# A second scratch bank in the half-product pairs, and token sums and squares spread over more of the down stage

## The chip, the cores and the metric

The kernel runs on one core of a Trainium2 chip. The metric is device time in microseconds (us) of one execution. A core has engines that each work through a queue of their own in order and wait for each other by semaphores: PE (TensorE) multiplies matrices and accumulates in PSUM, DVE (VectorE), ACT (ScalarE) and POOL (GpSimd) work on rows of 128 partitions, and SP (SyncE) does nothing here but issue DMA transfers. PSUM has eight banks of 128 x 512 float32 values.

## The reference, cut to what matters

The reference is one decoder layer on 512 tokens of width 1024: two token mixers (RWKV-7 and a sparse attention), their gated merge, and a feed-forward part. The change touches the feed-forward part alone, whose width D_FF is 2816:

```python
h = rms_norm(x, norm_ffn_pre)
u = causal_dwconv(h @ ffn_up, ffn_conv_w, ffn_conv_b)    # width 3, 2 x 2816 columns
u_gate, u_val = jnp.split(u, 2, axis=-1)
x = x + rms_norm((jax.nn.silu(u_gate) * u_val) @ ffn_down, norm_ffn_post)
```

Everything is float32 and agrees with the reference to float32's precision. To get this out of PE's faster number format, each operand is split into a high part and a low part (the rest), and a product is three matmuls: high by high, high by low, low by high.

## The kernel before

**The up stage** makes the 5632 columns of `h @ ffn_up` in 22 pairs j of two blocks of 128 columns, one of the gate and one of the value. Pairs 0 to 9 are plain products. Pairs 10 to 21 (`SEVEN`) go through `seven(j)`: the 2 x 2 grid of half-size products (two halves of the weights' rows and columns, two halves of the tokens) is made with seven products in place of eight. In it `prod` issues one product of 12 matmuls of 128 x 256 (line 1567), and `add` is a DVE operation (line 1572). Three PSUM banks hold a pair: g and v, which become the two blocks, and t, a scratch bank. With their numbers, the seven products go to: 1 g left, 2 t left, 3 v right, 4 t right, 5 g left (added to the first), 6 g right, 7 t right (added to the fourth). Between them DVE forms the sums: after product 2 the first one, `su` = t left - (copy of g left), by which t left is read for the last time; later v right = t right + `su4` after product 4; and v left = t right + `su` after product 7.

The tiles `pz` have two banks, used in turn; before the change a pair takes one of them, so that pairs 10, 12, 14 ... use one bank and 11, 13, 15 ... the other. Waits between engines on PSUM are kept by bank: a matmul into t right waits until a DVE operation that reads t left is done.

After each pair come the convolution on ACT and DVE (lines 1619 to 1621), SiLU, the product of both blocks, and the split of the result into `ah` (high, ACT) and `al` (low, DVE). The weights of later pairs are loaded by SP, and split by ACT (high, line 134) and POOL or DVE (low, line 172, tiles `sw...h` and `sw...l`), in program order between the rest.

**The down stage** does `@ ffn_down` for 256 tokens and 512 columns at a time, again with seven products in place of eight, m = 0 to 6. A call of `down(m, f, r, n, bank, side)` is one product: 11 steps k, each with one block of weights (loaded by SP and split by ACT, line 1668, and by DVE or POOL, line 1669) and six matmuls of 128 x 512 (lines 1733 to 1735). The blocks are numbered through: block dw(11 m + k) is step k of product m. A block is prepared ten steps ahead of its use. What runs beside the products is drawn in at the steps:

- `turn()` forms the token sums in place of the tokens as soon as these have been used. It is a generator with 15 steps: three loads of t24 from DRAM (1 MB, 1 MB and 0.75 MB; t24 was made in the up stage), then for each of three pieces (`TCH`: blocks 0 to 3, 4 to 7, 8 to 10) a difference of two DVE operations into `tt` (lines 1714, 1715) and a `put` (a copy on ACT, line 1701, and a rest on DVE, line 1702); then six more `put`s out of t24. The table `TURN` names, for each product m, the steps k that draw the next one.
- `side` is a second generator, drawn at each step k > 6: `copies` under product 1, `first_half` under product 2, `second_half` under product 5. `first_half(p2)` adds to the two banks of product 1 (line 1754), multiplies each with the norm's gain (`res`, line 1386), and takes its squares' sum on ACT (`p2jk`, line 1388), all through `stat`.
- Order is fixed by the program: what `keep` wraps is not moved by the scheduler, and every engine's queue is in order. So what a step draws in stands on DVE and ACT ahead of the weights' split of the block that is prepared there, ten steps ahead.

The token sums of rows 0, left, that the three pieces make are read by product 5; the first six `put`s out of t24 make what products 4 and 6 read.

Of the kernel before, what the change touches and what calls it, by code (L numbers as in the profile page):

```python
# [10 lines left out]
F32 = mybir.dt.float32  # L11
F32R = mybir.dt.float32r
AF = mybir.ActivationFunctionType
# [20 lines left out]
DCH = tuple(slice(i, min(i + 2, KH)) for i in range(0, KH, 2))  # L34
TURN = ((), (3, 8, 9), (0, 1, 3, 5, 7, 9), (2, 5, 8), (2, 5, 8), (), ())
TCH = (slice(0, 4), slice(4, 8), slice(8, 11))
# [16 lines left out]
def hybrid_layer(ctx: ExitStack, tc: tile.TileContext, a, out, dbg=None, stop=None):  # L53
# [33 lines left out]
    def pz(name):  # L87
        return pzs[-1][1].tile([128, 512], F32, tag="pz", name=name, bufs=2)
# [311 lines left out]
    p2 = lp[2]  # L400
# [1078 lines left out]
    with pool("ff") as ff:  # L1479
# [78 lines left out]
        def seven(j):  # L1558
# [14 lines left out]

            g, v, t = (pj if j % 2 else px)(f"sg{j}"), (pj if j % 2 else py)(f"sv{j}"), pz(f"st{j}")
            u2, u4 = (sw.tile([128, 256], F32, tag=f"u{i}", name=f"su{i}{j}", bufs=1) for i in (2, 4))
            prod(g[:, lft], tok(0, 0))
            prod(t[:, lft], forms[1])
            sc.activation(u2, g[:, lft], AF.Copy)
            add(u2, t[:, lft], u2, OP.subtract)
            prod(v[:, rgt], forms[0])  # L1580
            add(u4, v[:, rgt], u2)
            prod(t[:, rgt], forms[2])
            prod(g[:, lft], tok(1, 0), first=False)
            add(v[:, rgt], t[:, rgt], u4)
            prod(g[:, rgt], tok(1, 1))
            add(g[:, rgt], g[:, rgt], u4, OP.subtract)
            prod(t[:, rgt], forms[3], first=False)
            add(v[:, lft], t[:, rgt], u2)
            return g, v
# [90 lines left out]
        with pool("ep") as ep:  # L1680
# [23 lines left out]
            def turn():  # L1704
                def load(c):
                    keep(sy.dma_start(t24[:, c], t24d[c].rearrange("k p f -> p k f")))

                load(TCH[0])
                yield
                load(TCH[1])  # L1710
                yield
                for c in TCH:
                    x = ep.tile([128, 4, 256], F32, tag="tt", name=f"tt{c.start}", bufs=1)[:, :c.stop - c.start]
                    keep(ve.tensor_tensor(x, tok(ah, 0, 0, c).bitcast(F32), t24[:, c, lft], op=OP.subtract))
                    keep(ve.tensor_tensor(x, x, tok(al, 0, 0, c).bitcast(F32), op=OP.add))
                    yield
                    put(x, 0, 0, c)
                    yield
                    if c is TCH[0]:
                        load(TCH[2])  # L1720
                        yield
                for c in TCH:
                    put(t24[:, c, lft], 0, 1, c)
                    yield
                for c in TCH:
                    put(t24[:, c, rgt], 1, 0, c)
                    yield
# [8 lines left out]

            def down(m, f, r, n, bank, side=iter(())):
                p = [bank(f"dn{m}{i}") for i in range(2)]
                for k in range(KH - TL if m == 6 else KH):
# [5 lines left out]
                    if k % 3 == 0:  # L1745
                        next(ws, None)
                    if k > 6:
                        next(side, None)
# [12 lines left out]
            def first_half(p):  # L1761
                keep(sy.dma_start(g3, a["norms"][3:4, :].to_broadcast([128, D])))
                for i in range(2):
                    keep(add(p[i], p[i], pa[i]))
                    yield
                    s2[i] = stat(p[i], res2, i, g3, "p2", ep)
                    yield
# [13 lines left out]
            p5 = down(2, 0, 0, 1, pz, first_half(p2))  # L1781
            p4 = down(3, 3, 1, 1, pj)
            p = down(4, 1, 0, 1, px)
# [115 lines left out]
```

## Time and profile before

| | |
|---|---|
| median of 3 runs | 1147.31 us (1145.96 to 1150.28) |
| the profiled execution's own time | 1146.95 us |
| span in the profile, first to last instruction | 1144.9 us |
| mean granted TensorE clock | 0.998 |
| DVE, ACT, POOL busy | 747.6, 640.1, 608.5 us |
| chain that ended last: PE's share | 80% |
| DMA moved | 208.33 MB |

The span is divided into stages by the lines that PE executes. The twelve pairs in seven products run from 902.6 us to 1026.9 us, the down products from there to 1137.3 us, and what is left is the last norm and the stores. A row of the timeline has start, duration, engine, line, operation, the tile written and the tiles read, and in brackets the engine's idle time before it and what ended that. A row of the waits has who waited for whom, the sum in us, how many times, and the longest.

### The profile page before, as it was taken

The numbers are of one execution on the slowest core, as the hardware profiler recorded it, in microseconds if no ns is written. First come the engines' busy times: TensorE is split into PE (matmuls) and PEld (weight loads), VectorE is DVE, ScalarE is ACT, GpSimd is POOL, SyncE is SP. The second block draws the span as 40 slices with busy tenths as digits, with TensorE's granted clock in tenths as the row PEclk, the third lists the DMA queues.
The fourth block names the chain that finished last, engine by engine and source line by source line (L and its number), as shares of the span: only waits on it lengthen the run. The fifth ranks groups of instructions, "written<-read, shape, count | busy, mean of one in ns | idle before, by whom it ended". The sixth has DMA issues, their size and how long they took to land.

```text
span 1144.9 us, 21224 instructions
## 1 busy us (share of the span) xinstructions
PE 1116.2 (97%) x7704; PEld 910.2 (79%) x7704; DVE 747.6 (65%) x1432; ACT 640.1 (56%) x1258; POOL 608.5 (53%) x615
## 2 busy tenths in 40 slices
PE   9999999999999999999999999999999999999897
PEld 7888888877888877766677777888888889998685
DVE  4227664735665552597786754754885699997876
ACT  5547763554666334486665653543544666664644
POOL 4346674535666453476446544540677766753321
PEclk9999999999999999999999999999999999999999
DMA  7534468633666896426576556685658768968583
GB/s 240 149 86 123 139 168 212 180 102 96 177 144 169 233 256 207 113 71 194 170 209 181 126 126 200 212 289 146 176 160 215 223 223 230 265 185 310 168 288 117
DMA packets 117002, 208.33 MB, mean 182 GB/s; under 512 B 37025, under 2 KB 39905, under 8 KB 110754
## 3 DMA queue, kind: packets, MB, share of 16 engines
q1 hardware_dynamic: 93538, 144.05, 40.2%
q0 software_dynamic: 7504, 48.50, 18.3%
q10 hardware_dynamic: 15856, 14.42, 4.0%
q8 instruction: 61, 1.00, 0.4%
q14 instruction: 43, 0.35, 0.1%
HBM read 179.60 MB, written 72.35 MB: 220 GB/s over the span
## 4 chain that ended last, share of the span: by engine, by line
PE 80%; DVE 7%; DMA 4%; POOL 3%; issue 3%; ACT 2%; DVEq 0%; POOLq 0%; ACTq 0%; SPq 0%
PE sg L1567 4%; PE st L1567 4%; PE o L1218 3%; PE gt L348 3%; PE pt L150 3%; PE ub L1276 3%; PE pu L234 2%; PE gt L349 2%; PE ub L1278 2%; PE gt L350 2%; PE pu L233 2%; PE pu L232 2%; PE ub L1277 2%; PE v L348 2%; PE v L349 2%
## 5 line engine op out<-in xcount | busy, mean ns | idle before, releaser
L1166 ACT ACTIVATE p<-p,stt 128x384 f32<-128x384 f32 (+3 forms) x128 | 70.6, 554 | 33.5 <-DVE stt L1164 33.0
L1164 DVE CUSTOM_DVE_ANT_0 p<-s,rh 128x384 f32<-128x384 f32 (+3 forms) x128 | 59.2, 484 | 22.0 <-PE s L1150 18.4
L1734 PE MATMUL dn<-hl,ah 128*128 128x512 f32 x148 | 58.4, 394 | 2.1 <-DVE hl L1669 1.3
L1138 POOL TENSOR_SCALAR p<-p,stt 128x512 f32<-128x512 f32 (+1 forms) x64 | 39.7, 628 | 38.7 <-DVE stt L1131 23.9
L1735 PE MATMUL dn<-hh,al 128*128 128x512 f32 x148 | 57.7, 390 | 0.0
L1733 PE MATMUL dn<-hh,ah 128*128 128x512 f32 x148 | 56.4, 391 | 1.1 <-ACT hh L1668 1.1
L150 PE MATMUL pt<-ident,p 128*128 128x128 f32 x320 | 44.3, 273 | 1.3 <-DVE p L1140 1.2
L1157 PE MATMUL s<-kst,qs 128*128 128x512 f32 (+1 forms) x128 | 38.8, 394 | 6.4 <-DVE stt L1164 6.2
L150 PEld LDWEIGHTS pt<-ident,p 128*128 128x128 f32 x320 | 37.8, 141 | 7.1 <-DVE p L1140 1.6
L1218 PE MATMUL o<-PT,vt 128*64 128x384 f32 (+3 forms) x256 | 41.0, 443 | 0.0
L1734 PEld LDWEIGHTS dn<-hl,ah 128*128 128x128 f32 x148 | 27.8, 188 | 10.6 <-DVE hl L1669 3.6
L1733 PEld LDWEIGHTS dn<-hh,ah 128*128 128x128 f32 x148 | 27.6, 188 | 7.6 <-ACT hh L1668 2.0
L1157 PEld LDWEIGHTS s<-kst,qs 128*128 128x128 f32 x128 | 21.2, 189 | 15.5 <-DVE stt L1164 12.3
L1209 ACT ACTIVATE PT<-pt 128x512 f32<-128x512 f32 x48 | 27.5, 588 | 10.5 <-PE pt L150 10.3
L1140 DVE TENSOR_SCALAR p<-p,stt 128x512 f32<-128x512 f32 (+1 forms) x64 | 31.8, 524 | 0.7
L1735 PEld LDWEIGHTS dn<-hh,al 128*128 128x128 f32 x148 | 27.8, 188 | 5.5
L1218 PEld LDWEIGHTS o<-PT,vt 128*64 128x64 f32 x256 | 16.3, 136 | 18.3 <-issue 16.0
L272 POOL DMA_DIRECT2D ds<-in_down_dram x36 | 25.6, 711 | 7.6 <-DMA ds<-ds 7.6
L1620 DVE SCALAR_TENSOR_TENSOR u<-pu,cvec,u 128x511 f32<-128x511 f32 x20 | 15.0, 748 | 20.4 <-ACT u L1619 20.4
L1211 DVE COPY PT<-pt 128x512 f32<-128x512 f32 x32 | 21.8, 680 | 8.6 <-PE pt L150 8.5
L251 POOL DMA_DIRECT2D fs<-in_up_dram x36 | 26.1, 731 | 0.5 <-issue 0.4
L868 ACT ACTIVATE UV<-xs 64x256 f32<-64x256 f32 x16 | 6.1, 378 | 35.6 <-PE xs L861 35.2
(2203 smaller groups left out, 4237.8 us busy)
## 6 DMA issues: line engine op xcount, KB each, us to landing
fs<-in_up_dram POOLq DMA_DIRECT2D x36, 512.0 KB, 6.3
ds<-in_down_dram POOLq DMA_DIRECT2D x30, 512.0 KB, 6.3
fs<-fs POOLq DMA_DIRECT2D x12, 512.0 KB, 4.6
ds<-ds POOLq DMA_DIRECT2D x10, 512.0 KB, 5.5
gtd<-gt ACTq DMA_DIRECT2D x16, 256.0 KB, 4.5
qs<-qd SPq DMA_DIRECT2D x32, 128.0 KB, 4.3
g<-gtd SPq DMA_DIRECT2D x16, 256.0 KB, 3.6
t24d<-t SPq DMA_DIRECT2D x10, 256.0 KB, 5.4
```

The lines of the kernel that those rows point to most:

```text
L150: return te.transpose(o, i, ident)
L348: te.matmul(p, wh(k), hh[:, k, :], start=k == 0, stop=False)
L349: te.matmul(p, wh(k), hl[:, k, :], start=False, stop=False)
L1138: po.tensor_scalar(o.pe[e, b, k], o.pe[e, b, k], w, 1.0, op0=OP.mult, op1=OP.mult)
L1157: m = te.matmul(s_[:, :n], qt, kt[:, x, b, :n], start=x == 0, stop=x == 1)
L1164: ve.tensor_tensor_reduce(sb, parts[b], rh[e][:, (3 - qb) * 128:], -1.0, BIG, OP.add, OP.min, st[e][:, 0, i:i + 1])
L1166: sc.activation(sb, sb, AF.Exp, scale=-1.0, bias=st[e][:, 0, i:i + 1], accum_out=st[e][:, 1, i:i + 1])
L1218: te.matmul(acc[e * 64:e * 64 + 64, j * 128:], vt[:, j, b * 256 + g * 64:b * 256 + g * 64 + 64], m[e][:, c:c + n], start=False, stop=k == ...
L1567: te.matmul(p, w[y][:, ks], x[z][:, k, :], start=first and k + n == 0, stop=last and k == hf - 1 and n == 2, skip_group_check=True)
L1733: te.matmul(p, xh, w[0], start=first, stop=False)
L1734: te.matmul(p, xh, w[1], start=False, stop=False)
L1735: te.matmul(p, xl, w[0], start=False, stop=last)
```

## The change

In `seven` the scratch tile t becomes two tiles, t[0] for product 2 and t[1] for products 4 and 7, each a bank. Both banks of `pz` are now used by every pair.

In the down stage, `turn()` has another order: the difference and the `put` of the third piece (blocks 8 to 10) come after the first three `put`s out of t24 instead of before them. `TURN` draws the steps later: the first and second load under down product 1 at k = 6 and 10 instead of 3 and 8; the first piece's difference under product 2 at k = 1 instead of under product 1 at k = 9; the third load under product 2 at k = 5 instead of 1; the third piece's difference under product 3 at k = 9 and its `put` under product 4 at k = 1, instead of under product 2 at k = 7 and 9. The adds of `first_half` are made in one step and its two multiplications in two; the squares leave it and are drawn by a new generator, `squares`, under product 3 from k = 0 on. No operation is added or left out.

```diff
-TURN = ((), (3, 8, 9), (0, 1, 3, 5, 7, 9), (2, 5, 8), (2, 5, 8), (), ())
+TURN = ((), (6, 10), (1, 4, 5, 6, 10), (2, 5, 8, 9), (1, 3, 6, 9), (), ())
...
-            g, v, t = (pj if j % 2 else px)(f"sg{j}"), (pj if j % 2 else py)(f"sv{j}"), pz(f"st{j}")
+            g, v, t = (pj if j % 2 else px)(f"sg{j}"), (pj if j % 2 else py)(f"sv{j}"), [pz(f"st{j}{i}") for i in range(2)]
             prod(g[:, lft], tok(0, 0))
-            prod(t[:, lft], forms[1])
+            prod(t[0][:, lft], forms[1])
             sc.activation(u2, g[:, lft], AF.Copy)
-            add(u2, t[:, lft], u2, OP.subtract)
+            add(u2, t[0][:, lft], u2, OP.subtract)
             prod(v[:, rgt], forms[0])
             add(u4, v[:, rgt], u2)
-            prod(t[:, rgt], forms[2])
+            prod(t[1][:, rgt], forms[2])
             prod(g[:, lft], tok(1, 0), first=False)
-            add(v[:, rgt], t[:, rgt], u4)
+            add(v[:, rgt], t[1][:, rgt], u4)
             prod(g[:, rgt], tok(1, 1))
             add(g[:, rgt], g[:, rgt], u4, OP.subtract)
-            prod(t[:, rgt], forms[3], first=False)
-            add(v[:, lft], t[:, rgt], u2)
+            prod(t[1][:, rgt], forms[3], first=False)
+            add(v[:, lft], t[1][:, rgt], u2)
...
+                def diff(c):
+                    x[c.start] = y = ep.tile([128, 4, 256], F32, tag="tt", name=f"tt{c.start}", bufs=1)[:, :c.stop - c.start]
+                    keep(ve.tensor_tensor(y, tok(ah, 0, 0, c).bitcast(F32), t24[:, c, lft], op=OP.subtract))
+                    keep(ve.tensor_tensor(y, y, tok(al, 0, 0, c).bitcast(F32), op=OP.add))
...
+                diff(c0)
+                yield
+                put(x[c0.start], 0, 0, c0)
+                yield
+                load(c2)
+                yield
+                diff(c1)
+                yield
+                put(x[c1.start], 0, 0, c1)
+                yield
                 for c in TCH:
                     put(t24[:, c, lft], 0, 1, c)
                     yield
+                diff(c2)
+                yield
+                put(x[c2.start], 0, 0, c2)
+                yield
...
-            def down(m, f, r, n, bank, side=iter(())):
+            def down(m, f, r, n, bank, side=iter(()), at=7):
...
-                    if k > 6:
+                    if k >= at:
                         next(side, None)
...
                 for i in range(2):
                     keep(add(p[i], p[i], pa[i]))
+                yield
+                for i in range(2):
+                    keep(ve.tensor_tensor(res2[:, i, :], p[i], g3[:, 0:512], op=OP.mult))
                     yield
-                    s2[i] = stat(p[i], res2, i, g3, "p2", ep)
+
+            def squares(p):
+                for i in range(2):
+                    s2[i] = ep.tile([128, 3], F32, tag="p2ss", name=f"p2ss{i}", bufs=4)
+                    junk = ep.tile([128, 512], F32, tag="p2jk", name=f"p2jk{i}", bufs=1)
+                    keep(sc.activation(junk, p[i], AF.Square, accum_out=s2[i][:, 0:1]))
                     yield
...
-            p4 = down(3, 3, 1, 1, pj)
+            p4 = down(3, 3, 1, 1, pj, squares(p2), 0)
```

The order of the instructions on the engines shows this at three places. The first is PE in pair 11; the rows are the first matmul of products 2 to 7, `st` is the scratch tile (its number tells one tile from another), sg and sv are g and v. Before:

```order
L1567 MATMUL st_10122<-tf1h,sw112h 128x256
...
L1567 MATMUL sv_10121<-tf0h,sw111h 128x256 [waits Activation_49]
...
L1567 MATMUL st_10122<-tf2h,sw113h 128x256 [waits DVE_49]
...
L1567 MATMUL sg_10120<-hh,sw116h 128x256 [waits Activation_49]
...
L1567 MATMUL st_10122<-tf3h,sw118h 128x256 [waits DVE_49]
```

After the change, the same place:

```order
L1567 MATMUL st_10123<-tf1h,sw112h 128x256
...
L1567 MATMUL sv_10122<-tf0h,sw111h 128x256 [waits Activation_49]
...
L1567 MATMUL st_10124<-tf2h,sw113h 128x256 [waits DVE_49,Activation_49]
...
L1567 MATMUL sg_10121<-hh,sw116h 128x256 [waits Activation_49]
...
L1567 MATMUL st_10124<-tf3h,sw118h 128x256 [waits DVE_49]
```

Product 4 stands where it stood and still waits for DVE, but its tile is no longer that of product 2 (10124 against 10123). What it waits for on DVE is the last reader of its bank, which is now the last addition of the pair before, v left = t right + `su`.

The second place is ACT around the end of down product 2 (blocks dw27 to dw33; `tt` is a difference of tokens, `p2jk` a square). Before:

```order
L1668 ACTIVATE hh<-dw27r 128x512
L1701 ACTIVATE ah<-tt_12090 128x4x256
L1668 ACTIVATE hh<-dw28r 128x512
L1668 ACTIVATE hh<-dw29r 128x512
L1668 ACTIVATE hh<-dw30r 128x512
L1388 ACTIVATE p2jk_12152,p2ss_12150<-dn_11926 128x512
L1668 ACTIVATE hh<-dw31r 128x512
L1701 ACTIVATE ah<-tt_12135 128x3x256
L1668 ACTIVATE hh<-dw32r 128x512
L1388 ACTIVATE p2jk_12179,p2ss_12177<-dn_11927 128x512
L1668 ACTIVATE hh<-dw33r 128x512
```

After the change:

```order
L1668 ACTIVATE hh<-dw27r 128x512
L1668 ACTIVATE hh<-dw28r 128x512
L1668 ACTIVATE hh<-dw29r 128x512
L1668 ACTIVATE hh<-dw30r 128x512
L1668 ACTIVATE hh<-dw31r 128x512
L1668 ACTIVATE hh<-dw32r 128x512
L1701 ACTIVATE ah<-tt_12132 128x4x256
L1668 ACTIVATE hh<-dw33r 128x512
L1786 ACTIVATE p2jk_12195,p2ss_12194<-dn_11938 128x512
L1668 ACTIVATE hh<-dw34r 128x512
L1786 ACTIVATE p2jk_12208,p2ss_12207<-dn_11939 128x512
```

The two squares have moved behind dw33 and dw34, the second piece's copy behind dw32, and the third piece's copy (128x3x256) is gone from here; it now stands between dw45 and dw46.

The third place is DVE over the same blocks (`dn` is a bank of down product 1, `res` its product with the gain). Before:

```order
L1669 TENSOR_TENSOR hl<-dw27r,hh 128x512
L1702 TENSOR_TENSOR al<-tt_12090,ah 128x4x256
L1669 TENSOR_TENSOR hl<-dw29r,hh 128x512
L1714 TENSOR_TENSOR tt_12135<-ah,t_11852 128x768
L1715 TENSOR_TENSOR tt_12135<-tt_12135,al 128x768
L1754 TENSOR_TENSOR dn_11926<-dn_11926,pa_11848 128x512
L1669 TENSOR_TENSOR hl<-dw30r,hh 128x512
L1386 TENSOR_TENSOR res_11847<-dn_11926,gb_11853 128x512
L1702 TENSOR_TENSOR al<-tt_12135,ah 128x3x256
L1754 TENSOR_TENSOR dn_11927<-dn_11927,pa_11849 128x512
L1669 TENSOR_TENSOR hl<-dw32r,hh 128x512
L1386 TENSOR_TENSOR res_11847<-dn_11927,gb_11853 128x512
```

After the change:

```order
L1669 TENSOR_TENSOR hl<-dw27r,hh 128x512
L1712 TENSOR_TENSOR tt_12132<-ah,t_11864 128x1024
L1713 TENSOR_TENSOR tt_12132<-tt_12132,al 128x1024
L1669 TENSOR_TENSOR hl<-dw29r,hh 128x512
L1766 TENSOR_TENSOR dn_11938<-dn_11938,pa_11860 128x512
L1766 TENSOR_TENSOR dn_11939<-dn_11939,pa_11861 128x512
L1669 TENSOR_TENSOR hl<-dw30r,hh 128x512
L1779 TENSOR_TENSOR res_11859<-dn_11938,gb_11865 128x512
L1779 TENSOR_TENSOR res_11859<-dn_11939,gb_11865 128x512
L1669 TENSOR_TENSOR hl<-dw32r,hh 128x512
L1702 TENSOR_TENSOR al<-tt_12132,ah 128x4x256
L1669 TENSOR_TENSOR hl<-dw33r,hh 128x512
```

The third piece's three operations (128x768, 128x768, 128x3x256) are gone from here: its differences now stand between dw42 and dw44 and its rest between dw45 and dw47. The second piece's differences, which stood between dw24 and dw26, have come in. On SP the first load of t24 stood between dw14 and dw15 and now stands between dw17 and dw18, the second moved from ahead of dw20 to behind dw21, the third from ahead of dw24 to behind dw27.

More of the change, by code (lines that the diff above doesn't have):

```diff
@@ L1706, in load @@
                     keep(sy.dma_start(t24[:, c], t24d[c].rearrange("k p f -> p k f")))
-                load(TCH[0])
+                x = {}
+                def diff(c):
+                    x[c.start] = y = ep.tile([128, 4, 256], F32, tag="tt", name=f"tt{c.start}", bufs=1)[:, :c.stop - c.start]
+                    keep(ve.tensor_tensor(y, tok(ah, 0, 0, c).bitcast(F32), t24[:, c, lft], op=OP.subtract))
+                    keep(ve.tensor_tensor(y, y, tok(al, 0, 0, c).bitcast(F32), op=OP.add))
+                c0, c1, c2 = TCH
+                load(c0)
                 yield
-                load(TCH[1])
+                load(c1)
                 yield
[L1712 to L1721, printed above, removed]
+                diff(c0)
[8 more added lines that the diff above has]
+                yield
                 for c in TCH:
```

## The prediction

> **What bounds the kernel now.** I read the page's first lines, then the busy time by stage, then who waited for whom from 902 us on, then the timeline around the longest waits.
>
> ```profile
> span 1144.9 us, 21224 instructions
> PE 1116.2 (97%) x7704; PEld 910.2 (79%) x7704; DVE 747.6 (65%) x1432; ACT 640.1 (56%) x1258; POOL 608.5 (53%) x615
> 902.00:1033.00 131.00, 125.98 (x1040) 123.20 (x1039) 117.97 (x195) 85.61 (x148) 84.45 (x70) 1.00 0.76 225
> 1033.00:1055.00 22.00, 22.00 (x99) 18.22 (x98) 14.00 (x15) 9.81 (x17) 7.32 (x6) 1.00 0.98 344
> 1055.00:1080.00 25.00, 22.31 (x92) 16.33 (x91) 20.73 (x22) 13.70 (x25) 6.99 (x5) 1.00 0.56 174
> 1080.00:1105.00 25.00, 24.49 (x107) 19.57 (x106) 21.45 (x21) 16.17 (x27) 10.48 (x8) 1.00 0.84 294
> ```
>
> PE is busy for 97% of the span, so a change that takes no matmul away can win only PE's idle time. In the rows by stage (length, then busy us of PE, PEld, DVE, ACT, POOL, the granted clock, DMA's share, GB/s) PE is idle for 131.00 - 125.98 = 5.0 us among the pairs, 0 in the next stage, 25.00 - 22.31 = 2.7 us and 25.00 - 24.49 = 0.5 us in the down products. DVE is busy for 117.97 of 131.00, so 90% among the pairs: the engine that could take PE's place. The clock is 1.00 throughout.
>
> ```profile
> PE st L1567 <- DVE su L1572: 5.0, 6, 2.4
> PE dn L1734 <- DVE hl L1669: 1.3, 3, 0.6
> PE dn L1733 <- ACT hh L1668: 1.1, 2, 0.7
> PE dn L1734 <- POOL hl L1669: 0.6, 1, 0.6
> PEld st L1567 <- DVE su L1572: 6.6, 8, 2.5
> ```
>
> These waits are all of that idle time. The 5.0 us of the pairs is one wait: the fourth product, into scratch bank t, waits for the first subtraction `su`, which reads the other half of that bank. In the down products PE waits for weights that ACT, DVE or POOL split too late. The change is aimed at both.
>
> **What one wait costs.** The first matmuls of the fourth product in pair 10:
>
> ```profile
> 906.67 0.28 PE L1567 MATMUL sv<-tf0h,sw101l 128*128 128x256 f32 x1
> 908.32 0.39 PE L1567 MATMUL st<-tf2h,sw103h 128*128 128x256 f32 x1 [1.38 <-DVE su L1572]
> 908.55 0.28 PE L1567 MATMUL st<-tf2l,sw103h 128*128 128x256 f32 x1
> 908.66 0.28 PE L1567 MATMUL st<-tf2h,sw103l 128*128 128x256 f32 x1
> ```
>
> Without a wait, matmuls start 0.11 to 0.12 us apart (908.55 to 908.66). Here the starts are 1.65 and 0.23 us apart, which is 1.65 + 0.23 - 2 x 0.12 = 1.64 us lost with 1.38 us of idle time: 0.26 us more for starting up again. The weight loads waited 8 times, the matmuls 6. So the pairs lose 5.0 + 8 x 0.26 = **7.1 us**, and the down products, with six waits of matmuls, 3.2 + 6 x 0.26 = **4.8 us**. 11.9 us together is the most that the change can win.
>
> **The scratch bank.** The fourth product now has a bank whose last reader is the previous pair's last addition. That wait ends earlier than the old one, so the fourth product goes on at once. No operation is added. What is late next is the seventh product, which writes the same bank as the fourth and so waits for the third DVE addition, v right. What a pair keeps is therefore its old wait, or the time that this addition is ahead of the seventh product, whichever is less. Pairs 10, 11 and 12 on DVE and 12 on PE:
>
> ```profile
> 912.83 0.43 DVE L1572 TENSOR_TENSOR sg<-sg,su 128x256 f32<-128x256 f32 x1 [2.36 <-PE sg L1567]
> ...
> 920.85 0.68 DVE L172 TENSOR_TENSOR sw121l<-sw121r,sw121h 128x512 fp32r<-128x512 f32 x1
> ...
> 923.72 3.48 DVE L172 TENSOR_TENSOR sw128l<-sw128r,sw128h 128x512 fp32r<-128x512 f32 x1 [0.16 <-ACT sw128h L134]
> ...
> 934.33 0.42 DVE L1572 TENSOR_TENSOR sv<-st,su 128x256 f32<-128x256 f32 x1
> ```
>
> ```profile
> 930.96 0.39 PE L1567 MATMUL st<-tf2h,sw123h 128*128 128x256 f32 x1 [2.35 <-DVE su L1572]
> ...
> 935.21 0.28 PE L1567 MATMUL st<-tf3h,sw128h 128*128 128x256 f32 x1
> ```
>
> - *Pair 10*: after v right DVE stood idle for 2.36 us until the sixth product's sum was there. It has time to spare, and the whole 1.64 us is kept.
> - *Pair 12*: v right ends at 934.33 + 0.42 = 934.75, the seventh product starts at 935.21, so there are 0.46 us to spare against 2.35 + 0.26 = 2.61 us. 2.15 us of the wait come back ahead of the seventh product, and with its own start-up 0.2 us are kept. DVE is late here because of one weight split, 3.48 us where the same operation took 0.68 us at 920.85. POOL at that time:
>
> ```profile
> 923.55 0.52 POOL L272 DMA_DIRECT2D ds<-in_down_dram  x1
> 924.09 1.31 POOL L172 TENSOR_TENSOR sw124l<-sw124r,sw124h 128x512 fp32r<-128x512 f32 x1
> 925.35 1.29 POOL L172 TENSOR_TENSOR sw135l<-sw135r,sw135h 128x512 fp32r<-128x512 f32 x1
> ```
>
> DVE's subtraction ends 0.56 us after POOL's third piece of work in a row (926.64), as if it had been held until POOL paused. Every piece of this chain hangs on PE's progress, so it moves along with PE, and I take it to recur. The Trainium skill ("SBUF — State Buffer", section "Who interferes with whom") says that a VectorE instruction with two SBUF inputs and a GpSimd instruction that reads SBUF exclude each other, that whichever issues first holds the port for the whole instruction, and, as inferred there, that descriptor generation needs the write interface only. By that, this subtraction, begun while POOL was only issuing a DMA, would have gone through before 924.09; its row disagrees, and the measurement decides.
>
> - *The other six*: 5.0 - 1.38 - 2.35 = 1.27 us of idle time and 6 x 0.26 us of starts, 2.8 us together, some 0.5 us each. In pair 16:
>
> ```profile
> 974.78 0.42 DVE L1572 TENSOR_TENSOR sv<-st,su 128x256 f32<-128x256 f32 x1
> ...
> 975.75 0.28 PE L1567 MATMUL st<-tf3h,sw168h 128*128 128x256 f32 x1
> ```
>
> 0.55 us to spare (975.75 less 975.20), just enough; I take 2.5 of 2.8.
>
> Sum: 1.64 + 0.2 + 2.5 = **4.3 us**, between 0 (all of it turns up ahead of the seventh product) and 7.1. I take the value pair by pair since the rows give each.
>
> **The down stage.** Why blocks dw31 to dw33 were late, on ACT and DVE:
>
> ```profile
> 1069.19 0.60 ACT L1388 ACTIVATE p2jk<-dn 128x512 f32<-128x512 f32 x1 [5.09 <-DVE res L1386]
> ...
> 1069.78 0.62 ACT L1668 ACTIVATE hh<-dw31r 128x512 fp32r<-128x512 f32 x1
> ```
>
> ```profile
> 1057.26 1.79 DVE L1669 TENSOR_TENSOR hl<-dw24r,hh 128x512 fp32r<-128x512 f32 x1
> ...
> 1065.42 0.95 DVE L1714 TENSOR_TENSOR tt<-ah,t 128x768 f32<-128x768 f32 x1
> 1066.40 0.96 DVE L1715 TENSOR_TENSOR tt<-tt,al 128x768 f32<-128x768 f32 x1
> ```
>
> ACT stood for 5.09 us before a square that waits for DVE, with dw31's split queued behind it, and DVE was late because the third piece (0.95 + 0.96 us, and a rest of about as much) stood ahead of what the square needs. After the change the squares stand behind dw33 and dw34 and the third piece behind dw42. That takes 3 x 0.95 = 2.9 us from DVE's 20.73 of 25 us, leaving 17.9, and frees ACT. The 2.9 us go to the next 25 us, where DVE had 21.45: 24.3 of 25. That is tight, but spread from dw42 on. I let 0.5 us of wait return there or before dw30 to dw33, and take 4.8 - 0.5 = **4.3 us**, between 4.8 and -1 (if DVE falls behind by the 2.9 us and less than half of the 4.8 is won, with one more POOL split in the way).
>
> The loads of t24 matter only through what they cover:
>
> ```profile
> 1040.49 9.06 DMA dw20r<-in_down_dram
> ```
>
> In the chain of waits dw20 lands 9.06 us after its issue, behind the second 1 MB load, while DMA is 98% busy. PE now comes 4.3 us earlier, and so do the issues, which wait for buffers that PE and DVE free. The load's new place behind dw21 is the cover if they don't; without it I'd expect 1 to 2 us of waiting before dw20. I cost it at nothing.
>
> **Sum.** 1146.95 (the profiled execution) - 4.3 - 4.3 = 1138.35 us. That execution lies 0.36 us below the median of 1147.31, well within the three runs, so I predict **1138.3 us**, 0.8% less.
>
> **Rivals.**
> - *All waits go* (14%): DVE's held subtraction in pair 12 finds POOL in a pause, and nothing returns in the down products: 1146.95 - 7.1 - 4.8 = 1135.0 us. For it: the order of POOL and DVE shifts as pair 10 gets shorter by 1.6 us. Against: all of them hang on the same matmuls. It is also where the Trainium skill's rule, quoted above, would lead for pair 12.
> - *The wait only moves* (14%, with 3% of it for a wait of the fourth product that stays as it is): DVE, 90% busy, sets the pairs' pace, and each wait turns up ahead of the seventh product. Only the down stage pays: 1142.6 us. For it: 0.46 and 0.55 us to spare are little. Against: pair 10, and DVE's idle 13 us.
> - *The down waits only move* (9%): DVE's 24.3 of 25 us are too much, and dw42 to dw50 are late instead: 1146.95 - 4.3 = 1142.6 us.
> - *DVE is held more often* (4% slower by over 0.5%): PE runs on, so DVE's subtractions meet POOL's splits more often. A pair takes (1026.7 - 902.6) / 12 = 10.3 us now, and DVE has some 9.5 us of work in it (117.97 / 131.00 x 10.3 = 9.3, and what it must wait for). Two more splits of 1.3 us in its way per pair make 12.1 us: 12 x 1.8 = 21 us lost against 4.3 won below, 1164 us. It decides from about 1.7 us of added holding per pair on; 0.8 us would eat the whole gain of the pairs.
>
> **How the numbers follow.** The forecast with its unknowns of 1 to 2 us has 59%. About 0.5% (5.7 us) is what a measurement of this kernel can tell from no change: the line lies at 1141.6. Faster: 59% + 14% and a third of the two cases at 1142.6 = 0.80; within 0.5%: 0.16; slower 0.04. The range reaches from below the case in which all waits go to just past the cases at 1142.6: 1134 to 1143.5.
>
> **What would show it.** Right: no waits of `st` for `su`; PE idle among the pairs under 3 us, what is left being `st` (seventh product) waiting for `sv`, most of it in pair 12; the pairs' stage 4 us shorter; ACT's idle time before its first square short and dw31 to dw33 split before PE asks; PE idle between 1050 and 1080 under 1 us. Wrong: `st` waiting for `sv` in most pairs; weight loads waiting for dw42 to dw50; a wait for dw20 that ends with its landing.

## The result, and the profile after

The changed kernel took 1133.66 us (median of 4 runs, 1133.06 to 1135.97), the kernel before 1148.66 us (4 runs, 1145.96 to 1150.28): a ratio of 0.9875, 95% interval [0.9849, 0.9902]. Run again beside other runs of the kernel before it was 0.9903 [0.9886, 0.9921]. The profiled execution took 1133.54 us, with a span of 1131.5 us at a mean granted clock of 0.997. The page's first lines, then the rows by stage (length, busy us of PE, PEld, DVE, ACT, POOL, the granted clock, DMA's share, GB/s) for the pairs, for the down products and for 25 us within these, then the waits from the pairs on:

```profile
span 1131.5 us, 21237 instructions
PE 1110.3 (98%) x7704; PEld 909.6 (80%) x7704; DVE 750.4 (66%) x1432; ACT 639.2 (56%) x1258; POOL 613.5 (54%) x615
898.90:1019.00 120.10, 118.42 (x1010) 117.52 (x1009) 111.98 (x185) 80.28 (x141) 84.05 (x69) 1.00 0.79 235
1019.00:1123.90 104.90, 104.88 (x464) 86.52 (x462) 87.81 (x106) 59.45 (x105) 37.99 (x25) 1.00 0.69 235
1051.00:1076.00 25.00, 25.00 (x112) 20.71 (x111) 24.93 (x26) 15.20 (x27) 10.61 (x6) 1.00 0.66 203
```

```profile
PE st L1567 <- DVE sv L1572: 1.6, 3, 0.7
PEld st L1567 <- DVE sv L1572: 2.5, 4, 0.9
```

No wait of the fourth product for `su` is left, and none at all in the down products. What is left is the seventh product `st` waiting for the third addition `sv`: 1.6 us. DVE is busy for 111.98 of 120.10 us among the pairs (93%), and for 24.93 of 25.00 us in the down stage, and PE waits for nothing there.

Where the 13.4 us between the two spans went: the pairs are 4.1 us shorter, the down stage 5.7 us, the tail is the same, and **3.7 us lie ahead of the pairs**, in code that the change doesn't touch. The experiments had to settle that too.

### The profile page after: what moved, and what is told of

Its sections match the earlier page's. It is cut to its first block, busy times and chain, and to the rows that moved or that the text cites. A ratio compares the mean times of both kernels' runs of the same rounds, so it can differ in the third digit from the quotient of the medians.

```text
span 1131.5 us, 21237 instructions
## 1 busy us (share of the span) xinstructions
PE 1110.3 (98%) x7704; PEld 909.6 (80%) x7704; DVE 750.4 (66%) x1432; ACT 639.2 (56%) x1258; POOL 613.5 (54%) x615
## 4 chain that ended last, share of the span: by engine, by line
PE 87%; DVE 5%; DMA 3%; POOL 2%; issue 1%; ACT 1%; SPq 0%; DVEq 0%; POOLq 0%; ACTq 0%
PE st L1567 4%; PE sg L1567 3%; PE dn L1745 3%; PE dn L1746 3%; PE dn L1747 3%; PE gt L348 3%; PE o L1218 3%; PE gt L349 3%; PE gt L350 3%; PE pt L150 3%; PE ub L1276 3%; PE pu L234 2%; PE ub L1278 2%; PE pu L232 2%; PE pu L233 2%; PE ub L1277 2%
## 5 line engine op out<-in xcount | busy, mean ns | idle before, releaser
L1164 DVE CUSTOM_DVE_ANT_0 p<-s,rh 128x384 f32<-128x384 f32 (+3 forms) x128 | 59.2, 484 | 21.5 <-PE s L1150 17.9
L1209 ACT ACTIVATE PT<-pt 128x512 f32<-128x512 f32 x48 | 27.5, 587 | 10.4 <-PE pt L150 10.3
```

What stands on the lines that cost most here:

```text
L1164: ve.tensor_tensor_reduce(sb, parts[b], rh[e][:, (3 - qb) * 128:], -1.0, BIG, OP.add, OP.min, st[e][:, 0, i:i + 1])
```

## The experiments

All profiles in one table. Pairs: from the first matmul of pair 10 (`sg` of `sw105h`) to the first of the down products; down: from there to the start of its last matmul; idle is PE's. A ratio is to the kernel before, run on the same chip; where there is none, the kernel was profiled once and not timed in rounds.

| kernel | ratio, 95% interval | pairs begin | pairs (idle) | down (idle) |
|---|---|---|---|---|
| before | | 902.6 | 124.2 (5.0) | 110.2 (3.2) |
| before again | | 900.0 | 126.9 (7.3) | 109.3 (2.6) |
| down stage only | 0.9952 [0.9934, 0.9969] | 900.9 | 125.5 (6.0) | 104.5 (0.0) |
| bank only | 0.9958 [0.9934, 0.9982] | 899.2 | 122.9 (4.4) | 110.7 (3.1) |
| changed | 0.9875 [0.9849, 0.9902] | 898.9 | 120.1 (1.7) | 104.5 (0.0) |
| changed again | 0.9903 [0.9886, 0.9921] | 900.2 | 121.6 (3.0) | 104.5 (0.0) |
| bank and squares only | | 899.9 | 121.4 (2.9) | 107.7 (2.6) |
| changed, squares as before | | 903.2 | 119.9 (1.9) | 104.5 (0.0) |
| changed, loads as before | | 900.1 | 118.9 (1.0) | 104.9 (0.0) |
| before, one DMA issue moved | 0.9976 [0.9959, 0.9992] | 898.4 | 123.6 (4.3) | 110.5 (3.1) |
| changed, third product's split on POOL | 0.9936 [0.9915, 0.9956] | 899.2 | 122.5 (4.1) | 104.5 (0.0) |
| changed, third addition first | 0.9927 [0.9901, 0.9953] | 899.2 | 124.8 (5.5) | 104.5 (0.0) |
| changed, both: addition, DMA issues | 0.9919 [0.9892, 0.9945] | 901.5 | 120.1 (2.2) | 104.5 (0.0) |
| changed, DMA issues moved | 0.9923 [0.9906, 0.9939] | 902.2 | 122.1 (3.7) | 104.6 (0.0) |

And the length of each pair (us, from first matmul to first matmul); a pair without waits takes 9.7:

| pair | 10 | 11 | 12 | 13 | 14 | 15 | 16 | 17 | 18 | 19 | 20 | 21 |
|---|---|---|---|---|---|---|---|---|---|---|---|---|
| before | 11.4 | 10.3 | 12.4 | 9.7 | 10.2 | 10.1 | 10.5 | 10.0 | 9.7 | 10.5 | 9.8 | 9.7 |
| before again | 11.4 | 10.4 | 12.3 | 9.7 | 10.2 | 10.3 | 9.9 | 12.4 | 10.2 | 10.8 | 9.8 | 9.7 |
| down stage only | 11.4 | 10.4 | 12.3 | 9.7 | 10.2 | 10.1 | 10.1 | 10.0 | 9.7 | 11.2 | 10.8 | 9.7 |
| one DMA issue moved | 11.5 | 10.3 | 10.5 | 9.7 | 10.2 | 10.1 | 11.4 | 10.0 | 9.7 | 10.9 | 9.8 | 9.7 |
| bank only | 9.7 | 9.8 | 9.8 | 9.7 | 9.9 | 10.4 | 10.7 | 10.6 | 9.7 | 12.3 | 10.7 | 9.8 |
| changed | 9.7 | 9.8 | 9.8 | 9.7 | 9.9 | 10.1 | 10.4 | 10.6 | 9.7 | 9.9 | 10.8 | 9.8 |
| changed again | 9.7 | 9.8 | 9.8 | 9.7 | 9.9 | 10.1 | 10.4 | 10.8 | 9.7 | 11.3 | 10.7 | 9.8 |
| split on POOL | 11.3 | 9.8 | 10.5 | 9.7 | 9.8 | 9.8 | 9.7 | 11.5 | 9.7 | 10.6 | 9.9 | 10.5 |
| third addition first | 9.7 | 9.8 | 9.8 | 9.7 | 9.8 | 10.8 | 11.5 | 11.5 | 10.1 | 10.9 | 10.8 | 10.6 |
| both | 9.7 | 9.8 | 9.8 | 9.7 | 9.8 | 9.8 | 9.7 | 9.8 | 9.7 | 10.3 | 10.7 | 11.6 |
| DMA issues moved | 9.7 | 9.8 | 9.8 | 9.7 | 9.8 | 9.8 | 10.9 | 10.8 | 10.7 | 10.7 | 10.7 | 9.8 |

### Each part alone, and both kernels again

Bank only: `seven` as changed (this line, and the uses of `t` that follow from it), the down stage as before. The down stage only: the other way round.

```diff
-            g, v, t = (pj if j % 2 else px)(f"sg{j}"), (pj if j % 2 else py)(f"sv{j}"), pz(f"st{j}")
+            g, v, t = (pj if j % 2 else px)(f"sg{j}"), (pj if j % 2 else py)(f"sv{j}"), [pz(f"st{j}{i}") for i in range(2)]
```

> Only the second product's own bank; the down stage is that of before. Pairs' stage: 120.1 us against 124.1 (no wait of st for su, some 1.7 us of idle time before the seventh product), down stage 110.6 as before. Total 4.1 us below the kernel before (ratio 0.9964) by the theory that each part pays what its own stage shows, and that the 3.7 us by which the pairs began earlier in the changed kernel come from variation between executions. Rival, that the bank change itself makes everything ahead of the pairs faster: the pairs begin at 899 us and the total is 7.7 us below.

> Only the down stage's new order; the pairs share the bank as before. Down stage 104.9 us against 110.6, no wait of PE left in it; pairs 124.1 with 5.0 us idle for su. Total 5.7 us below the kernel before (ratio 0.9950). Rival, that the down stage ran without waits only because the pairs ended in another rhythm: 107 to 110 us for the down stage, and the total 1 to 3 us below.

> The changed kernel once more, on the chip of the two runs above. If the parts add up: 9.8 us below the kernel before (ratio 0.9914), pairs 120.1, down 104.9, and the pairs begin anywhere between 898 and 904 us. If they help one another: more than the sum of the two runs above by over 2 us.

> The kernel before once more: what varies between executions ahead of the pairs. By the theory of variation the pairs begin somewhere else than at 902.6 us, by one to four us, while pairs (124.1) and down stage (110.6) stay within 0.7 us. By the rival they begin at 902.6 again.

The parts add up: 0.9958 x 0.9952 = 0.9910, and both together 0.9903. The down stage gives 104.5 us with either form of the pairs. The pairs themselves vary by 3 to 4 us between executions of the same code: 124.2 to 126.9 us with the shared bank in three profiles, 118.9 to 122.9 us with the new one in six (means 125.5 and 120.8). So bank only, at 122.9 us, missed its forecast of 120.1 by what executions differ in; where its loss sits is pair 19, read below. The kernel before, run again, missed its forecast as well: 126.9 and 109.3 us, where 124.1 and 110.6 were to hold within 0.7. Its pair 17 took 12.4 us, and 2.03 us of that is the seventh product waiting for `sv`: the wait that the new bank leaves over comes up with the shared bank too.

The pairs began at 898.4 to 903.2 us over the fourteen profiles, and at 902.6 and 900.0 us in two executions of the kernel before. The rows that differ are the very first. From 5 to 15 us, in the kernel before, then in the kernel before again:

```profile
5.00:10.00 5.00, 5.00 (x10) 1.95 (x10) 2.25 (x10) 3.13 (x7) 0.56 (x1) 1.00 1.02 356
10.00:15.00 5.00, 5.00 (x18) 3.61 (x17) 3.27 (x5) 2.82 (x6) 1.98 (x2) 1.00 1.05 380
```

```profile
5.00:10.00 5.00, 4.30 (x15) 2.22 (x14) 3.08 (x11) 3.66 (x9) 0.42 (x1) 0.85 0.97 342
10.00:15.00 5.00, 5.00 (x27) 3.73 (x26) 3.19 (x6) 4.08 (x9) 3.42 (x3) 0.81 1.06 385
```

The same program began 25 matmuls in one execution and 39 in the other (a row counts those as well that run across its bounds). Five of the fourteen profiles, of five different kernels, start in the slower way (10 matmuls from 5 to 10 us), have their hundredth matmul at 23.1 to 23.6 us, and begin the pairs at 900.9 to 903.2 us, mean 902.1; nine start in the faster way (15), have it at 21.1 to 21.7 us, and begin the pairs at 898.4 to 900.2 us, mean 899.5. So the 3.7 us ahead of the pairs are not the change's: some 2.6 us go with the way of starting, the rest was not taken apart.

### What made the down stage shorter

Three kernels take its parts apart. In the first the squares stand among the fourth product's blocks, as changed (and the adds and multiplications ahead of them as changed too), while loads and pieces stand as before, with the old `turn()`; in the second it is the squares, adds and multiplications that stand as before; in the third only the two first loads do.

```diff
-TURN = ((), (6, 10), (1, 4, 5, 6, 10), (2, 5, 8, 9), (1, 3, 6, 9), (), ())
+TURN = ((), (3, 8, 9), (0, 1, 3, 5, 7, 9), (2, 5, 8), (2, 5, 8), (), ())
...
```

```diff
...
-            p4 = down(3, 3, 1, 1, pj, squares(p2), 0)
+            p4 = down(3, 3, 1, 1, pj)
```

```diff
-TURN = ((), (6, 10), (1, 4, 5, 6, 10), (2, 5, 8, 9), (1, 3, 6, 9), (), ())
+TURN = ((), (3, 8), (1, 4, 5, 6, 10), (2, 5, 8, 9), (1, 3, 6, 9), (), ())
```

> The bank of the changed kernel, and of the down stage only the squares moved from the third to the fourth product; loads and pieces of the token sums stand as before. Theory of the prediction: ACT's idle time before the first square (5.09 us with dw31's split behind it) is most of the loss, so PE idle in the down stage falls from 3.2 to about 1 us, and the stage from 110.5 to 106.5 us. Rival, that the third piece ahead of dw30 to dw36 is the loss: idle over 2 us, stage over 108 us.

> The changed kernel with the squares back behind each product by g3, in the third product's last blocks; loads and pieces as changed. Theory of the prediction: ACT still stands before the square, since the square waits for the sum and the product on DVE, and about 1 us of idle time is left at dw31 to dw33, stage 106 us. Rival, that DVE alone was late: no idle time, 104.5 us.

> The changed kernel with the two 1 MB loads of t24 behind dw14 and dw19 as before, instead of behind dw17 and dw21. The prediction's cover: dw20 lands some 9 us after its issue and PE, now early, waits 1 to 2 us ahead of it, stage 106 us. Rival, that the blocks are far enough ahead: no wait, 104.5 us, dw20's slack down by 3 us and nothing else.

The rival came out with the second and third kernel. The first lies between: 2.6 us of idle time, as the rival said, but 107.7 us, under the rival's 108 and over the theory's 106.5. DVE's timeline there, PE's longest wait, and ACT:

```profile
1059.88 2.04 DVE L1714 TENSOR_TENSOR tt<-ah,t 128x768 f32<-128x768 f32 x1
1061.96 0.96 DVE L1715 TENSOR_TENSOR tt<-tt,al 128x768 f32<-128x768 f32 x1
1062.84 1.29 DVE L1754 TENSOR_TENSOR dn<-dn,pa 128x512 f32<-128x512 f32 x2
1064.04 0.68 DVE L1669 TENSOR_TENSOR hl<-dw30r,hh 128x512 fp32r<-128x512 f32 x1
```

```profile
1064.89 0.50 PE L1733 MATMUL dn<-hh,ah 128*128 128x512 f32 x1 [2.17 <-ACT hh L1668]
```

```profile
1062.95 0.84 ACT L1701 ACTIVATE ah<-tt 128x768 fp32r<-128x768 f32 x1 [3.87 <-DVE tt L1715]
...
1064.22 0.61 ACT L1668 ACTIVATE hh<-dw33r 128x512 fp32r<-128x512 f32 x1
```

The wait ends with ACT's split of dw33 (1064.22 + 0.61 = 1064.83): by the count of matmuls the one that waits is the next product's first, put ahead of those that read dw30's low half. ACT came to dw33 late because it had stood for 3.87 us ahead of its copy of the third piece (`tt` of 128x768), until DVE had that piece. DVE's split of dw30, which PE needs right after, ended at 1064.04 + 0.68 = 1064.72, behind the same piece and the sums. On either path the third piece on DVE comes first; that it is this one, and not the two pieces before it, is read from these rows and wasn't tried alone. Still, the squares' new place alone shortens the stage by some 3 us: 107.7 us where the bank alone takes 110.7, with 3 waits of weight loads in place of 12. With the pieces moved and the squares as before, ACT's timeline is this:

```profile
1061.39 0.60 ACT L1388 ACTIVATE p2jk<-dn 128x512 f32<-128x512 f32 x1 [5.46 <-DVE res L1386]
...
1061.98 0.62 ACT L1668 ACTIVATE hh<-dw31r 128x512 fp32r<-128x512 f32 x1
```

ACT stands for 5.46 us ahead of the square, with dw31 queued behind it, longer than the 5.09 us of the kernel before, and PE waits for nothing: dw31's low half is there 1.5 us before PE asks. So with the pieces moved, an idle engine with work queued behind it costs nothing, and the squares' new place adds nothing: 104.5 us with it or without. What the two moves win overlaps: the pieces alone win the whole, the squares alone about half. The early loads cost 0.4 us at most (104.9 against 104.5) and no wait at dw20: it landed 8.9 us after its issue instead of 5.6, and its low half still had 2.6 us to spare. The cover that the prediction asked for wasn't needed.

### What makes pair 12 long

In all three profiles with the shared bank and DMA issues as they were, pair 12 took 12.3 to 12.4 us, and DVE's subtraction `sw128l` 3.37 to 3.48 us; in all with the new bank 9.8 us where DVE's splits weren't moved. DVE's split and POOL in the changed kernel:

```profile
917.83 0.82 DVE L172 TENSOR_TENSOR sw128l<-sw128r,sw128h 128x512 fp32r<-128x512 f32 x1 [0.16 <-ACT sw128h L134]
```

```profile
916.67 1.43 POOL L172 TENSOR_TENSOR sw126l<-sw126r,sw126h 128x512 fp32r<-128x512 f32 x1 [1.55 <-ACT sw126h L134]
918.05 0.52 POOL L272 DMA_DIRECT2D ds<-in_down_dram  x1
918.58 1.31 POOL L172 TENSOR_TENSOR sw124l<-sw124r,sw124h 128x512 fp32r<-128x512 f32 x1
```

Now it begins 0.22 us before POOL's DMA issue; in the kernel before it began 0.17 us after (923.72 and 923.55). Both times it begins some 0.56 us before the pair's first matmul (923.72 and 924.29; 917.83 and 918.39), but POOL's `sw126l` is 0.4 us later against PE (2.10 us ahead, then 1.72). To test this, in the kernel before one DMA issue was moved on POOL, from between `sw126l` and `sw124l` to behind `sw135l`:

```diff
+            if j == 12:
+                next(ws, None)
...
-                if (j > 2 or x == 0 if j < SEVEN[0] else x == 0 and j < 19):
+                if (j > 2 or x == 0 if j < SEVEN[0] else x == 0 and j < 19 and j != 11):
```

> The kernel before, with one edit: the DMA issue that stands on POOL between the splits sw126l and sw124l stands behind sw135l. Theory from the rows so far (all four subtractions of 3.4 to 3.7 us began 0.17 to 0.27 us after such an issue did, with two splits queued directly behind it): DVE's subtraction sw128l then takes 0.7 to 1.9 us, pair 12 takes 9.8 to 10.3 us instead of 12.3, and the kernel is some 2.2 us faster than before, with the scratch bank still shared. Rival, that sw128l is long because three splits of POOL come close together, with or without the issue: 3 us or more, and pair 12 stays at 12.3 us.

```profile
919.60 1.58 DVE L172 TENSOR_TENSOR sw128l<-sw128r,sw128h 128x512 fp32r<-128x512 f32 x1 [0.16 <-ACT sw128h L134]
```

```profile
919.34 1.29 POOL L172 TENSOR_TENSOR sw124l<-sw124r,sw124h 128x512 fp32r<-128x512 f32 x1
920.96 1.38 POOL L172 TENSOR_TENSOR sw135l<-sw135r,sw135h 128x512 fp32r<-128x512 f32 x1 [0.32 <-ACT sw135h L134]
```

1.58 us, and pair 12 takes 10.5 us (9.8 to 10.3 were forecast), 1.8 to 1.9 less, with the bank still shared. So pair 12's gain is not the bank's alone: what the bank changed there is the moment at which DVE meets POOL. The opposite case came up by itself in the bank-only kernel, at pair 19. DVE and POOL, then the seventh product:

```profile
988.79 3.66 DVE L172 TENSOR_TENSOR sw198l<-sw198r,sw198h 128x512 fp32r<-128x512 f32 x1 [0.17 <-ACT sw198h L134]
```

```profile
988.54 0.78 POOL L272 DMA_DIRECT2D ds<-in_down_dram  x1
989.08 1.56 POOL L172 TENSOR_TENSOR sw194l<-sw194r,sw194h 128x512 fp32r<-128x512 f32 x1
990.34 1.55 POOL L172 TENSOR_TENSOR sw205l<-sw205r,sw205h 128x512 fp32r<-128x512 f32 x1
```

```profile
1000.08 0.39 PE L1567 MATMUL st<-tf3h,sw198h 128*128 128x256 f32 x1 [2.09 <-DVE sv L1572]
```

Begun 0.25 us after the issue, held through both splits, and pair 19 takes 12.3 us where the changed kernel has 9.9. The new bank didn't help: the wait turned up ahead of the seventh product.

### What holds the pairs at 10 to 11 us in the second half

In pairs 15, 16, 17 and 20 the seventh product waits in both profiles of the changed kernel (in pair 15 its weight load alone, 0.2 us). DVE ahead of the third addition of pair 16, and POOL:

```profile
962.33 0.41 DVE L1572 TENSOR_TENSOR su<-st,su 128x256 f32<-128x256 f32 x1
...
963.59 1.76 DVE L172 TENSOR_TENSOR sw171l<-sw171r,sw171h 128x512 fp32r<-128x512 f32 x1
965.27 0.68 DVE L1639 TENSOR_TENSOR al<-sv,ah 128x512 fp32r<-128x512 f32 x1
965.88 0.41 DVE L1647 TENSOR_TENSOR t<-sv,ah 128x256 f32<-128x256 f32 x1
966.21 0.41 DVE L1572 TENSOR_TENSOR sv<-st,su 128x256 f32<-128x256 f32 x1
```

```profile
963.49 1.31 POOL L172 TENSOR_TENSOR sw173l<-sw173r,sw173h 128x512 fp32r<-128x512 f32 x1
```

```profile
966.68 0.39 PE L1567 MATMUL st<-tf3h,sw168h 128*128 128x256 f32 x1 [0.35 <-DVE sv L1572]
```

The split begins 0.10 us behind one of POOL's and takes 1.76 us instead of 0.68; al and t follow, then the addition. In the kernel before, pair 16 had this long split too:

```profile
970.92 0.42 DVE L1572 TENSOR_TENSOR su<-st,su 128x256 f32<-128x256 f32 x1
...
972.18 1.75 DVE L172 TENSOR_TENSOR sw171l<-sw171r,sw171h 128x512 fp32r<-128x512 f32 x1
```

From the first subtraction to the third addition DVE took 3.86 us there (the addition at 974.78) and takes 3.88 us now. So DVE isn't slower than before; PE, which waited 0.43 us ahead of the fourth product then and waits no more, comes earlier to the seventh. Four kernels tried to take this away: the split goes to POOL; the addition ahead of al and t; that with the DMA issues moved; the DMA issues moved alone.

```diff
-                for x, eng in (((0, 0), po), (2, po), (1, ve), (3, po), ((0, 1), po), (4, po), ((1, 1), ve)):
+                for x, eng in (((0, 0), po), (2, po), (1, po), (3, po), ((0, 1), po), (4, po), ((1, 1), ve)):
```

```diff
-            add(v[:, rgt], t[1][:, rgt], u4)
+            keep(ve.tensor_tensor(v[:, rgt], t[1][:, rgt], u4, op=OP.add))
+            while late:
+                rest(*late.pop())
...
-            ve.tensor_tensor(al[:, j, :], y, ah[:, j, :].bitcast(F32), op=OP.subtract)
...
+            if j in SEVEN and j < 21:
+                late.append((j, y))
+            else:
+                rest(j, y)
```

```diff
             prod(v[:, rgt], forms[0])
+            if j > SEVEN[0] and j < 20:
+                next(ws, None)
...
-                if (j > 2 or x == 0 if j < SEVEN[0] else x == 0 and j < 19):
+                if j < SEVEN[0] and (j > 2 or x == 0):
```

Here `rest` holds the low half `al` and the token differences `t` of the pair before, unchanged.

> The changed kernel, with the low half of the third product's weights (sw101 to sw211) split on POOL instead of DVE. Theory: what is left among the pairs comes back ahead of the seventh product because the third addition stands behind that split, which POOL's own splits stretch from 0.68 to 1.75 us. Without it the waits of st for sv fall below 0.5 us, the pairs take 117 to 118 us (the two runs of the changed kernel: 120.1 and 121.6), and the ratio to the kernel before is 0.987 or less. Rival: POOL, with 12 x 1.3 = 16 us more on its 84 of 120, now has four splits in a row, holds DVE's other subtractions longer or delivers late, and the pairs take 121 us or more. A third, that the third addition is late because DVE as a whole is 93% busy: 119 us, since only 12 x 0.7 us go.

> The changed kernel, with the previous pair's low half (al) and token differences (t) put on DVE behind the third addition instead of ahead of it, pairs 11 to 21. Theory: what came back ahead of the seventh product is DVE's order, 0.68 + 0.41 us too much ahead of the third addition; pairs 15, 16, 17, 20 go from 10.1 to 10.8 down to 9.7 to 9.9 us, waits of st for sv fall to those behind late landings (under 1 us), pairs 117 to 119 us (six runs with the new bank: 118.9 to 122.9, mean 120.8), ratio to the kernel before 0.987 or less. Rival, that DVE has no time to give: what is put off makes sg or the next pair's subtraction late, and the pairs stay at 120 to 123 us.

> The kernel of the run above, with the nine DMA issues of POOL among the pairs put behind the first split of the next pair, where POOL then waits for ACT. Theory: no subtraction of DVE is over 2 us any more, pairs 117 to 118.5 us, ratio 0.986. Rival, that the moved issues only meet other subtractions, or their transfers other loads (the weights of pair 19 landed 8.8 us after issue): a subtraction of over 2 us elsewhere or more idle time behind landings, 120 us or more.

> The changed kernel with the nine DMA issues of POOL moved behind the first split of the next pair, and DVE's order as it is. Theory: the long subtractions (3.66 us in pair 19 of the bank alone, 2.3 us lost there) can't come up any more, the subtractions of 1.75 us in pairs 15, 16, 17 and 20 stay, since these begin 0.1 us behind a split and not behind an issue; pairs 119 to 121 us, ratio 0.990, the same as the changed kernel. Rival, that the issues were what shifts POOL against DVE in each pair: those subtractions fall to 0.68 us too, pairs 117 to 118.5 us, ratio 0.987 or less.

None beat the changed kernel, and the theory that DVE's order alone is the loss fell. Two of them, the third addition first (124.8 us) and the DMA issues moved (122.1 us), lie outside what their theory and their rival named. With the split on POOL other operations are held, the worst in pair 10 by three splits in a row behind a DMA issue:

```profile
902.16 4.42 DVE L1630 TENSOR_TENSOR u<-u,u 128x512 f32<-128x512 f32 x1
```

```profile
901.69 0.52 POOL L272 DMA_DIRECT2D ds<-in_down_dram  x1
902.22 1.31 POOL L172 TENSOR_TENSOR sw115l<-sw115r,sw115h 128x512 fp32r<-128x512 f32 x1
903.47 1.30 POOL L172 TENSOR_TENSOR sw112l<-sw112r,sw112h 128x512 fp32r<-128x512 f32 x1
904.73 1.29 POOL L172 TENSOR_TENSOR sw111l<-sw111r,sw111h 128x512 fp32r<-128x512 f32 x1
```

With the addition ahead, `t` comes 0.1 us later against POOL. In pair 17 of the changed kernel, then of that one:

```profile
977.14 0.41 DVE L1648 TENSOR_TENSOR t<-t,al 128x256 f32<-128x256 f32 x1
```

```profile
977.05 0.79 POOL L272 DMA_DIRECT2D ds<-in_down_dram  x1
```

```profile
981.05 2.19 DVE L1608 TENSOR_TENSOR t<-t,al 128x256 f32<-128x256 f32 x1
```

```profile
980.84 0.79 POOL L272 DMA_DIRECT2D ds<-in_down_dram  x1
981.39 1.56 POOL L172 TENSOR_TENSOR sw184l<-sw184r,sw184h 128x512 fp32r<-128x512 f32 x1
```

Begun 0.09 us after the issue it takes 0.41 us, begun 0.21 us after it 2.19 us: a tenth of a microsecond in the order costs 1.8 us, and pairs 16 and 17 take 11.5 us. With the DMA issues out of that place as well, pairs 11 to 18 all run at 9.7 to 9.8 us, which is what the theory wanted, but pairs 19 to 21 lose 3.5 us again. In the last kernel pairs 11 to 15 run at 9.7 to 9.8 us with the splits at 0.68 us, and pairs 17 to 20 at 10.7 to 10.8 with each of them at 1.75 or 1.76: two rhythms of the same code. What moves it from one to the other wasn't settled. Late landings are one candidate: in the changed kernel's second run ACT stood 3.10 us ahead of the split of `sw196r`, which landed 8.8 us after its issue, and pair 19 took 11.3 us; in the first run it landed after 7.4 us, and pair 19 took 9.9. It wasn't tried by itself.

## Why the prediction was right, and where it was wrong

It said 1138.3 us, 8.6 below the profiled execution of before, with 1134 to 1143.5 as its range. The median of 1133.66 us lies 4.6 us below that and just under the range, nearest to the rival in which all waits go (1135.0). The change's own stages gave 4.1 + 5.7 = 9.8 us; the 13.4 us of the two spans have 3.7 us in them that belong to neither kernel. Without those the changed kernel would stand at 1137.2, a microsecond from the forecast.

- *The scratch bank: 4.3 predicted, 4.1 measured* between the two profiles first compared, 4.7 between the means of three and six. The mechanism holds: no wait for `su`, what is left is the seventh product waiting for the third addition. But two of its terms were wrong and cancelled, so that 4.3 met 4.1 is luck. By pair, from 12 rows of either kernel: pair 10 kept 1.69 (predicted 1.64, right). Pair 12 kept 2.61, where the step "Every piece of this chain hangs on PE's progress, so it moves along with PE, and I take it to recur" gave 0.2: DVE's piece moved with PE, POOL's came 0.4 us later against it, and the hold was gone in every profile of the changed kernel. *The other six* were to keep 2.5 of 2.8; the remaining ten pairs together kept -0.2, since what pairs 11 to 19 saved (0.9) was lost again in pairs 20 and 21 (1.1). The 0.55 us to spare in pair 16, "just enough", was read from a chain in which the wait itself had given DVE time: the wait with its start-up was 0.43 + 0.26 = 0.69 us, DVE takes as long as before, and the pair kept 0.12 us.
- *The down stage: 4.3 predicted, 5.7 measured.* The step that failed is the bound of 4.8: it counted the six waits of matmuls for the starts lost, though the pairs had been counted by waits of weight loads. Those of the kernel before:

```profile
PEld dn L1734 <- DVE hl L1669: 3.6, 5, 1.0
PEld dn L1733 <- ACT hh L1668: 2.0, 2, 1.1
PEld dn L1734 <- POOL hl L1669: 1.4, 3, 1.1
```

 Ten: 3.2 + 10 x 0.26 = 5.8 us, and 5.7 were won. By the same count the five other profiles with waits in this stage come to 4.9, 6.2, 6.0, 3.4 and 0.3 us, and they are 4.8, 6.2, 6.0, 3.2 and 0.4 us longer than the 104.5 of the changed kernel. The 0.5 us that should return did not, though DVE was not relieved as the sum has it: 17.9 of 25 us were to be left and 24.3 in the next 25, and it was busy for 24.93 from 1051 on and for 21.43 in the next. The second piece's differences have come in there, and splits of 0.68 us took up to 1.78; no block came late all the same. Of the two reasons given, DVE's pieces alone win the whole; that the squares' place frees ACT wins some 3 us without them and nothing beside them.
- *The loads* were costed at nothing, which is right, though not for their new place: without it they cost nothing that PE waits for.
- *The rivals.* "All waits go" was right for pair 12 and the down stage. "The wait only moves" was right for pairs 16, 17 and 20. "DVE is held more often" did not come with this change, but did with two of the experiments, the split on POOL and the third addition first: the pairs took 2 to 4 us more than the mean of 120.8.
- *The signs named* came as listed (ACT's idle time before its first square is 1.42 us, after 5.09), but for one: most of the wait that is left was to be in pair 12, and it is in pairs 16, 17 and 20.

The Trainium skill's rule ("SBUF — State Buffer", "Who interferes with whom"), that a VectorE instruction with two SBUF inputs and a GpSimd one that reads SBUF exclude each other for a whole instruction by order of issue, was read as contradicted by the 3.48 us of before. Where no DMA issue is near, the rows agree with the rule (0.10 us behind a split DVE's took 1.76 us, and POOL's next one 1.76 us instead of 1.3). Next to an issue they agree only if the splits behind it get their turn some 0.1 to 0.2 us after the issue's start, ahead of their own recorded starts, and keep it through two or three in a row; that is an inference from the rows, not shown, so whether the rule holds there stays open. The course that the prediction drew from the rule for pair 12, no hold, is the one that came, but not for its reason: DVE began 0.22 us ahead of the issue, and not during it.

## What to carry to other kernels

When an engine at 90% load takes over the pace, read what is late next from the pairs where it already had no time, and don't count a wait's own length as time to spare. Count lost starts by the waits of the weight loads, stage by stage in the same way. Before blaming an idle engine ask how long PE could do without what stands behind it, and try each of two suspects both alone and beside the other: here what they win overlaps. Compare stages over several executions before a microsecond is put down to an edit: here the same code differed by up to 4 us in one stage.

## What the runs showed of the hardware that was not expected

- A subtraction on DVE with both inputs in SBUF that began 0.17 to 0.47 us after a POOL DMA issue, with splits of POOL queued behind that, took until these were through: 3.37, 3.37, 3.48 and 3.66 us behind two, 4.42 us behind three, 2.17 to 2.19 us behind one. Begun 0.07 to 0.10 us after the issue, such took 0.41 us. Those with one input in PSUM were not held: `sg<-sg,su` begun 0.34 us after an issue took 0.43 us, and `t<-sv,t` begun 0.37 us after one 0.42 us.
- One program starts in two ways: 25 or 39 matmuls begun from 5 to 15 us, though the granted clock of the slower start reads 1.00 and that of the faster one 0.85 and 0.81. The pairs begin 2.6 us later on average after the slower one, which came in 5 of 14 profiles whatever the kernel.
- Pairs of the same code repeat one length several times in a row (9.7 to 9.8 us nine times, 10.7 to 10.9 us five times, 11.5 us twice). That the order in which DVE's and POOL's operations meet sets it fits the rows; it was not shown.
